# One first load in place of two, and the first casts dealt out anew, in a fused LoRA kernel

## The chip, the core and the metric

The kernel runs on one core of a Trainium2 chip. The metric is the device time of one execution in microseconds (us). Before the change it is 123.47 us, the median of 3 runs (123.42 to 123.6).

The engines are called as the profile calls them: PE (TensorE, matrix products), DVE (VectorE), ACT (ScalarE), POOL (GpSimd) and SP (SyncE, which here only issues DMAs and waits). PEld is the loading of weights on PE. Sixteen DMA engines move data between the chip's memory (HBM) and the core's on-chip memory.

## The reference

```python
def setup_inputs():
    batch, seq, d_model, r = 16, 512, 768, 16
    ...
def reference(x, A, B, scale):
    lora = np.matmul(np.matmul(x, A), B)
    return (x + scale * lora).astype(np.float32)
```

x is 8192 rows of 768 float32 numbers (25.2 MB), A is 768 x 16, B is 16 x 768, scale is 0.5. The result has the shape of x. So 25.2 MB come in and as many go out, and the arithmetic between is small: two products over a rank of 16, and one addition.

## The kernel before, in words

**Tiles.** The 8192 rows are 64 tiles of 128 rows. `PARTS = [9, 7, 16, 16, 16]` deals them into five parts; in a part of S tiles, each of the 128 partitions holds S rows that lie one behind the other in HBM, so a transfer of n tiles moves n x 3072 bytes in one piece per partition. `x_all` has room for the first 48 tiles in float32; the last part (16 tiles) takes the place of parts 0 and 1 when their results have been stored. The sum is made in place in `x_all`, and stored from there.

**Groups.** Compute goes in 8 groups of 8 tiles. In each group:

1. ACT and POOL cast ("narrow") four tiles each from float32 `x_all` to float16 `xn` (`narrowed`, line 194). ACT takes the first four tiles of a group, POOL the last four. In the first group this is dealt otherwise: POOL casts tiles 0 and 1, ACT tiles 2 and 3, then tiles 4 to 7.
2. DVE turns `xn` into `xt` (`turned`, line 250): a transpose of 32 x 32 blocks, so that the model dimension comes to lie across partitions. One instruction turns all eight tiles; in the first group there are two of four tiles each.
3. PE multiplies `xt` by A's weights `w_bd` into `ps_yt` (`projected`, line 281, 24 matmuls).
4. ACT scales that into `y_bd` (line 238, four instructions).
5. PE multiplies `y_bd` by B's weights `b_mm` into `lora_ps` (`raised`, line 302), for four pairs of tiles.
6. DVE adds each pair to `x_all` (`summed`, line 255, four instructions).

PE's program overlaps neighbouring groups, and semaphores tie the engines together. `s_first` and `s_narrow` count casts, `s_turned` turns, `s_y` and `s_spread` the steps 3 and 4, `s_lora` finished pairs. ACT casts its tiles of the next group (line 234) before it does step 4 of the present one, and the casts wait until PE has begun to read the turned tiles of the group before (`s_taken`).

**Weights.** A comes by three small DMAs into 12 rows of `a_rows`, DVE turns them (`a_t`, line 243), POOL casts them into `w_one` (line 214) and copies that four times into the block weights `w_bd` (line 220). B comes by one DMA into every fourth row of `b_rows`. POOL casts it to `b_half` (line 212). PE spreads it with the matrix `pick` (line 315, two matmuls, before anything else on PE), and ACT casts the result to `b_mm` (line 231). DVE's wait ahead of line 243 is on `s_a`, which counts A's three loads and POOL's cast of tiles 0 and 1. PE's first projection waits for `w_bd` (`s_w`, line 320) and then for the turned group (`s_turned`, line 321).

**Transfers.** All DMAs are issued by SP, in the order of its program, on one queue. `LOADS` lists the loads of x as (part, first tile, tiles). SP issues loads 0 and 1, waits until POOL has cleared `a_rows` (line 153), issues A's three, waits until POOL has cleared `b_rows`, issues B's, and then loads 2 to 5 without a wait. Each load has a semaphore of its own, and a cast waits for the load that its tiles come by. The first store (9 tiles, line 170) waits for ten finished pairs of tiles (line 169), though its sums are done earlier; the second (7 tiles) goes with it. The two loads of part 4 wait until these stores have landed (lines 172 to 175). The store of part 2 waits for the sixth group's step 5 to begin (`s_raise`, line 181); the last two stores wait for their sums.

Of the kernel before, what the change touches and what calls it, by code (L numbers as in the profile page):

```python
# [18 lines left out]
SUB = 4  # L19
# [5 lines left out]
SETS, SET = 3, 4  # L25
# [3 lines left out]
def kernel(  # L29
# [25 lines left out]
    def sb(name, shape, dtype):  # L55
        return nc.alloc_sbuf_tensor(name, shape, dtype).ap()
# [13 lines left out]
    b_rows = sb("b_rows", [P, D], fp32)  # L70
    b_half = sb("b_half", [P, D], MM_DT)
# [11 lines left out]
    def sem(name):  # L83
        sems.append(nc.alloc_semaphore(name))
        return sems[-1]
# [10 lines left out]
    def memory(t2, i, s, n):  # L96
        S = PARTS[i]
        return t2[ds(parts[i], S * P), :].rearrange("(p s) d -> p s d", s=S)[:, ds(s, n), :]

    def held(i, s, n):  # L100
        return tiles(where.index((i, s)), n)

    def tiles(t, n):
        return x_all[:, ds(t % ROOM, n), :]

    LOADS = [
        (0, 0, 2), (0, 2, 7), (1, 0, 7), (2, 0, 8), (2, 8, 8), (3, 0, 16), (4, 0, 8), (4, 8, 8)
    ]
    s_load = [sem(f"s_load{k}") for k in range(len(LOADS))]

    def load_of(t):
        i, s = where[t]
        return next(k for k, ld in enumerate(LOADS) if ld[0] == i and ld[1] <= s < ld[1] + ld[2])

    assert SETS * SET == NC
    s_a, s_b = sem("s_a"), sem("s_b")
    s_ready, s_brows, s_pick = sem("s_ready"), sem("s_brows"), sem("s_pick")
    s_w, s_bh, s_bp, s_bm = sem("s_w"), sem("s_bh"), sem("s_bp"), sem("s_bm")
    s_first, s_narrow, s_turned, s_taken = sem("s_first"), sem("s_narrow"), sem("s_turned"), sem("s_taken")
# [16 lines left out]
    def on_sync(e):  # L136
        def load(k):
            ld = LOADS[k]
            e.dma_start(out=held(*ld), in_=memory(x2, *ld)).then_inc(s_load[k], 16)  # L139

        def summed(k):
            e.wait_ge(s_sum, sorted(set(STORED)).index(STORED[k]) + 1)
            if STORED[k] + 1 < NG:

                e.sem_inc(s_free[PAIRS - 1], 1)

        def store(k, done):
            st = STORES[k]
            e.dma_start(out=memory(out2, *st), in_=held(*st)).then_inc(done, 16)

        load(0)
        load(1)
        e.wait_ge(s_ready, 1)
        blocks = A.rearrange("(c e) r -> c (e r)", e=64)
        for c in range(SETS):
            e.dma_start(
                out=a_rows[c : SET * SET : SET, :], in_=blocks[ds(c * SET, SET), :]
            ).then_inc(s_a, 16)
        e.wait_ge(s_brows, 1)
        e.dma_start(out=b_rows[0 : R * APART : APART, :], in_=B).then_inc(s_b, 16)  # L160
        for k in range(2, len(LOADS) - 2):
            load(k)

        for p in range(2, PAIRS):
            e.sem_inc(s_free[p], 1)
        summed(0)


        e.wait_ge(s_lora, 2 * PAIRS + 2)
        store(0, s_out0)  # L170
        store(1, s_out1)
        e.wait_ge(s_out0, 16)
        load(len(LOADS) - 2)
        e.wait_ge(s_out1, 16)
        load(len(LOADS) - 1)
        for k in range(2, len(STORES)):
            summed(k)
            if k == 2:


                e.wait_ge(s_raise, 6)
            store(k, s_out)
# [3 lines left out]
    def narrowed(e, copy, g, first, n=SUB):  # L186
        t = g * GROUP + first
        for k in dict.fromkeys(load_of(t + k) for k in range(n)):
            if (e, k) not in here:
                here.add((e, k))  # L190
                e.wait_ge(s_load[k], 16)
        if g:
            e.wait_ge(s_taken, g)
        ins = copy(out=xn[:, ds(first, n), :], in_=tiles(t, n))  # L194

        ins.then_inc(s_narrow if g else s_first if first else s_a, 1)

    def on_gpsimd(e):
        e.memset(a_rows[0:Q], 0.0).then_inc(s_ready, 1)  # L199
        e.memset(b_rows, 0.0).then_inc(s_brows, 1)  # L200
        e.memset(pick, 0.0).then_inc(s_pick, 1)
        e.memset(w_bd.rearrange("p c k m -> p (c k m)").bitcast(fp32), 0.0)  # L202
        e.memset(y_bd.rearrange("p s m -> p (s m)").bitcast(fp32), 0.0).then_inc(s_ready, 1)  # L203
        e.wait_ge(s_pick, 1)
        e.affine_select(  # L205
            out=pick, in_=pick, compare_op=mybir.AluOpType.not_equal, fill=1.0, base=0,
            pattern=[[0, NQ], [-APART, Q]], channel_multiplier=1,
        ).then_inc(s_pick, 1)
        narrowed(e, e.tensor_copy, 0, 0, SUB // 2)
        e.wait_ge(s_pick, 2)  # L210
        e.wait_ge(s_b, 16)
        e.tensor_copy(out=b_half, in_=b_rows).then_inc(s_bh, 1)  # L212
        e.wait_ge(s_ready, 3)
        e.tensor_copy(  # L214
            out=w_one.rearrange("i (c e) k r -> i c e (k r)", c=SETS),
            in_=a_t[0:Q].rearrange("i k r (e c) -> i c e (k r)", c=SET)[:, 0:SETS, 0:SET, :],
        ).then_inc(s_w, 1)
        e.wait_ge(s_w, 1)
        for b in range(NQ):
            e.tensor_copy(  # L220
                out=w_bd[ds(b * Q, Q), :, :, ds(b * Q, R)], in_=w_one
            ).then_inc(s_w, 1)
            e.wait_ge(s_w, b + 2)
        for g in range(1, NG):
            narrowed(e, e.tensor_copy, g, SUB)

    def on_scalar(e):
        narrowed(e, e.copy, 0, SUB // 2, SUB // 2)
        narrowed(e, e.copy, 0, SUB)
        e.wait_ge(s_bp, 1)  # L230
        e.copy(out=b_mm, in_=lora[0][:, 0, :]).then_inc(s_bm, 1)  # L231
        for g in range(NG):
            if g + 1 < NG:
                narrowed(e, e.copy, g + 1, 0)
            e.wait_ge(s_y, g + 1)
            for b in range(NQ):
                q = ds(b * Q, Q)
                last = e.mul(out=y_bd[q, :, q], in_=y_ps[q, :, :], mul=sc)  # L238
            last.then_inc(s_spread, 1)

    def on_vector(e):
        e.wait_ge(s_a, SETS * 16 + 1)
        e.transpose(  # L243
            out=a_t[0:Q].rearrange("i k r c -> i (k r) c"),
            in_=a_rows[0:Q].rearrange("c (i k r) -> c (k r) i", k=2, r=R),
        ).then_inc(s_ready, 1)

        def turned(first, n):
            ts = [v[:, ds(first, n), :].bitcast(fp32) for v in (xt, xn)]
            return e.transpose(out=ts[0], in_=ts[1])  # L250

        def summed(g, p):
            xs = tiles(g * GROUP + 2 * p, 2)
            e.wait_ge(s_lora, g * PAIRS + p + 1)
            ins = e.tensor_tensor(out=xs, in0=xs, in1=lora[p % 2], op=mybir.AluOpType.add)  # L255
            if p + 1 == PAIRS and g in STORED:
                ins.then_inc(s_sum, 1)
            elif g + 1 < NG or p + 2 < PAIRS:
                ins.then_inc(s_free[p], 1)

        for h in range(2):
            e.wait_ge(s_first, h + 1)
            ins = turned(h * SUB, SUB)
        ins.then_inc(s_turned, 1)
        for g in range(NG):
            if g + 1 < NG:
                e.wait_ge(s_y, g + 1)
                e.wait_ge(s_narrow, 2 * (g + 1))  # L268
                turned(0, GROUP).then_inc(s_turned, 1)
            for p in range(PAIRS):  # L270
                summed(g, p)

    def on_tensor(e):
# [58 lines left out]
        for p in range(PAIRS):  # L332
            raised(p)

    on_sync(nc.sync)
    on_gpsimd(nc.gpsimd)
    on_scalar(nc.scalar)
    on_vector(nc.vector)
    on_tensor(nc.tensor)

# [43 lines left out]
```

## Time and profile before

| what | value |
|---|---|
| time, median of 3 runs | 123.47 us (123.42 to 123.6) |
| time of the profiled execution | 123.43 us |
| its span, first to last instruction | 121.6 us |
| mean granted PE clock | 0.91 |
| busy: PE, PEld | 49.8 us (41%), 29.2 us (24%) |
| busy: DVE, ACT, POOL | 81.7 us (67%), 37.4 us (31%), 28.4 us (23%) |
| HBM read, HBM written | 25.26 MB, 25.17 MB |
| DVE sums (line 255) | 32 of 1735 ns, 53.7 us |
| DVE turns of x (line 250) | 9, 27.1 us |
| ACT casts of x (line 194) | 9, 23.4 us |
| POOL casts of x (line 194) | 8, 20.7 us |

The profile is one execution. The span runs from the first to the last recorded instruction; the time of the execution is some 1.8 us longer. An engine's busy time is that of its instructions, without waits. The profile has a list of the costliest groups of instructions (line, engine, operation, what is written from what, how many), a chain of waits that is followed back from the last instruction, a list of the instructions in order of time, and tables that give busy time, DMA share and GB/s for any stretch of the span. In rows of the list in order of time, the first number is the start in us from the span's beginning, the second the length in us, and what stands in square brackets is how long the engine had been idle and what ended that.

### The profile page before, as it was taken

Reading aid. Unit: us, or ns where it says so; the run is one execution under the profiler, and the core shown is the slowest. Engines: PE = TensorE matmul, PEld = TensorE weight load, DVE = VectorE, ACT = ScalarE, POOL = GpSimd, SP = SyncE. Lnnn points to the kernel's source line nnn. Section 1 sums busy time; section 2 is a strip of 40 time slices with the busy share of each in tenths; the row PEclk is TensorE's granted clock in tenths of the full one; section 3 lists DMA queues with packets and bytes.
Section 4 is the critical chain, followed back from the end, with each engine's and each line's share of the span. In section 5 each row is a group of like instructions: output and inputs, shape, how many; then the busy total and the mean of one; then the engine's idle time right before and its main releaser. Section 6 shows DMA issues by size and latency. Waiting matters only on the chain.

```text
span 121.6 us, 884 instructions
## 1 busy us (share of the span) xinstructions
PE 49.8 (41%) x322; PEld 29.2 (24%) x322; DVE 81.7 (67%) x42; ACT 37.4 (31%) x43; POOL 28.4 (23%) x24
## 2 busy tenths in 40 slices
PE   0000209487457547746745734774674320000000
PEld 0000006253223424424423322442442110000000
DVE  0000970599999999999999989999995990000000
ACT  4000967626408312735340093643004000000000
POOL 7730567126009002605300080620000000000000
PEclk9999999999999999999999999999999995555555
DMA  3999999999999897999999999998999899899890
GB/s 63 437 431 457 446 398 469 404 420 469 437 517 420 356 517 336 427 421 410 446 416 436 428 428 485 420 517 372 404 517 404 372 517 404 372 517 404 372 517 0
DMA packets 1928, 50.43 MB, mean 415 GB/s; under 512 B 236, under 2 KB 236, under 8 KB 392
## 3 DMA queue, kind: packets, MB, share of 16 engines
q1 hardware_dynamic: 1928, 50.43, 97.0%
HBM read 25.26 MB, written 25.17 MB: 415 GB/s over the span
## 4 chain that ended last, share of the span: by engine, by line
DVE 33%; DMA 29%; PE 9%; ACT 6%; POOL 2%; issue 2%; SPq 0%; DVEq 0%
DVE x_sb L255 21%; DMA x_sb<-in_x_dram 20%; DVE xt L250 12%; DMA out_dram<-x_sb 9%; PE ps_yt L281 6%; ACT xn L194 3%; PE lora_ps L302 3%; ACT y_bd L238 2%; POOL xn L194 2%; SPq L139 0%; SPq L379 0%; DVEq L268 0%; SPq L134 0%
## 5 line engine op out<-in xcount | busy, mean ns | idle before, releaser
L255 DVE TENSOR_TENSOR x_sb<-x_sb,lora_ps 128x1536 f32<-128x1536 f32 x32 | 53.7, 1735 | 1.4 <-PE lora_ps L302 1.4
L194 ACT CAST xn<-x_sb 128x3072 f16<-128x3072 f32 (+1 forms) x9 | 23.4, 2609 | 35.9 <-DMA x_sb<-in_x_dram 24.8
L302 PE MATMUL lora_ps<-b_mm,y_bd 128*128 128x512 f16 (+1 forms) x128 | 25.0, 328 | 22.6 <-ACT y_bd L238 14.3
L194 POOL CAST xn<-x_sb 128x3072 f16<-128x3072 f32 (+1 forms) x8 | 20.7, 2586 | 43.9 <-DMA x_sb<-in_x_dram 24.6
L250 DVE STREAM_TRANSPOSE xt<-xn 128x3072 f32<-128x3072 f32 (+1 forms) x9 | 27.1, 3006 | 5.3 <-PE ps_yt L281 4.4
L281 PE MATMUL ps_yt<-xt,w_bd 128*128 128x256 f16 x192 | 25.2, 282 | 12.2 <-DVE xt L250 12.2
L281 PEld LDWEIGHTS ps_yt<-xt,w_bd 128*128 128x128 f16 x192 | 18.5, 99 | 19.7 <-issue 15.4
L302 PEld LDWEIGHTS lora_ps<-b_mm,y_bd 128*128 128x128 f16 x128 | 10.6, 97 | 35.5 <-ACT y_bd L238 16.6
L238 ACT ACTIVATE y_bd<-ps_yt 32x256 f16<-32x256 f32 x32 | 12.0, 374 | 18.7 <-PE ps_yt L281 18.4
L243 DVE STREAM_TRANSPOSE a_t<-a_rows 32x1024 f32<-32x1024 f32 x1 | 2.0, 1955 | 12.2 <-DMA a_rows<-in_A_dram 12.2
L315 PE MATMUL lora_ps<-b_half,pick 128*128 128x512 f16 (+1 forms) x2 | 0.8, 500 | 13.5 <-POOL b_half L212 13.5
L315 PEld LDWEIGHTS lora_ps<-b_half,pick 128*128 128x128 f16 x2 | 0.1, 105 | 13.5 <-issue 13.5
L212 POOL CAST b_half<-b_rows 128x768 f16<-128x768 f32 x1 | 0.8, 827 | 5.5 <-DMA b_rows<-in_B_dram 5.5
L220 POOL COPY w_bd<-w_one 32x384 f16<-32x384 f16 x4 | 2.0, 500 | 0.2
L194 ACT ACT_TABLE_LOAD x1 | 1.3, 1283 | 0.9 <-SPq L134 0.9
L202 POOL MEMSET w_bd<- 128x1536 f32 x1 | 1.4, 1372 | 0.0
L214 POOL CAST w_one<-a_t 32x384 f16<-32x384 f32 x1 | 0.9, 857 | 0.9 <-DVE a_t L243 0.9
L199 POOL MEMSET a_rows<- 32x1024 f32 x1 | 0.9, 941 | 0.5 <-SPq L134 0.5
L231 ACT CAST b_mm<-lora_ps 128x768 f16<-128x768 f32 x1 | 0.8, 798 | 0.0
L200 POOL MEMSET b_rows<- 128x768 f32 x1 | 0.7, 728 | 0.0
L203 POOL MEMSET y_bd<- 128x512 f32 x1 | 0.5, 514 | 0.0
L205 POOL TENSOR_SCALAR_AFFINE_SELECT pick<-pick 128x128 f16<-128x128 f16 x1 | 0.3, 298 | 0.0
(5 smaller groups left out, 0.6 us busy)
## 6 DMA issues: line engine op xcount, KB each, us to landing
out_dram<-x_sb SPq DMA_DIRECT2D x3, 6144.0 KB, 20.1
x_sb<-in_x_dram SPq DMA_DIRECT2D x4, 3072.0 KB, 17.6
x_sb<-in_x_dram SPq DMA_DIRECT2D x1, 6144.0 KB, 41.6
x_sb<-in_x_dram SPq DMA_DIRECT2D x2, 2688.0 KB, 12.4
out_dram<-x_sb SPq DMA_DIRECT2D x1, 3456.0 KB, 11.5
out_dram<-x_sb SPq DMA_DIRECT2D x1, 2688.0 KB, 17.7
x_sb<-in_x_dram SPq DMA_DIRECT2D x1, 768.0 KB, 4.5
a_rows<-in_A_dram SPq DMA_DIRECT2D x3, 16.0 KB
```

The costliest lines, as they stand in the source:

```text
L194: ins = copy(out=xn[:, ds(first, n), :], in_=tiles(t, n))
L199: e.memset(a_rows[0:Q], 0.0).then_inc(s_ready, 1)
L202: e.memset(w_bd.rearrange("p c k m -> p (c k m)").bitcast(fp32), 0.0)
L214: e.tensor_copy(out=w_one.rearrange("i (c e) k r -> i c e (k r)", c=SETS), in_=a_t[0:Q].rearrange("i k r (e c) -> i c e (k r)", c=SET)[:, ...
L220: e.tensor_copy(out=w_bd[ds(b * Q, Q), :, :, ds(b * Q, R)], in_=w_one).then_inc(s_w, 1)
L238: last = e.mul(out=y_bd[q, :, q], in_=y_ps[q, :, :], mul=sc)
L243: e.transpose(out=a_t[0:Q].rearrange("i k r c -> i (k r) c"), in_=a_rows[0:Q].rearrange("c (i k r) -> c (k r) i", k=2, r=R),).then_inc(s_r ...
L250: return e.transpose(out=ts[0], in_=ts[1])
L255: ins = e.tensor_tensor(out=xs, in0=xs, in1=lora[p % 2], op=mybir.AluOpType.add)
L281: mm = e.matmul(y_ps, w_bd[:, c, k, :], xv[:, :, c, :, k], start=(m == 0), stop=(m == MMS - 1),)
L302: mms.append(e.matmul(t[:, k, ds(n0, w)], y_bd[:, 2 * p + k, :], b_mm[:, ds(n0, w)], start=True, stop=True,))
L315: last = e.matmul(lora[0][:, 0, ds(n0, w)], pick.rearrange("p b r -> p (b r)"), b_half[:, ds(n0, w)], start=True, stop=True,)
```

## The change

Four things are edited.

- `LOADS` begins with one load of nine tiles, (0, 0, 9), in place of (0, 0, 2) and (0, 2, 7). SP issues it, then goes on as before.
- The first group is cast like the others: ACT tiles 0 to 3, POOL tiles 4 to 7, one instruction each. The first of DVE's two turns waits for ACT's cast (`s_first`), the second for POOL's, which now counts on `s_narrow`; so the later waits on `s_narrow` are one higher.
- The cast of `b_rows` to `b_half` moves from POOL to ACT, behind ACT's cast of tiles 0 to 3.
- DVE's wait ahead of the turn of A counts A's three loads alone.

```diff
     LOADS = [
-        (0, 0, 2), (0, 2, 7), (1, 0, 7), (2, 0, 8), (2, 8, 8), (3, 0, 16), (4, 0, 8), (4, 8, 8)
+        (0, 0, 9), (1, 0, 7), (2, 0, 8), (2, 8, 8), (3, 0, 16), (4, 0, 8), (4, 8, 8)
     ]
...
         load(0)
-        load(1)
         e.wait_ge(s_ready, 1)
...
-        for k in range(2, len(LOADS) - 2):
+        for k in range(1, len(LOADS) - 2):
             load(k)
...
-        ins.then_inc(s_narrow if g else s_first if first else s_a, 1)
+        ins.then_inc(s_narrow if g or first else s_first, 1)
...
     def on_gpsimd(e):
...
-        narrowed(e, e.tensor_copy, 0, 0, SUB // 2)
-        e.wait_ge(s_pick, 2)
-        e.wait_ge(s_b, 16)
-        e.tensor_copy(out=b_half, in_=b_rows).then_inc(s_bh, 1)
+        narrowed(e, e.tensor_copy, 0, SUB)
         e.wait_ge(s_ready, 3)
...
     def on_scalar(e):
-        narrowed(e, e.copy, 0, SUB // 2, SUB // 2)
-        narrowed(e, e.copy, 0, SUB)
+        narrowed(e, e.copy, 0, 0)
+        e.wait_ge(s_b, 16)
+        e.copy(out=b_half, in_=b_rows).then_inc(s_bh, 1)
         e.wait_ge(s_bp, 1)
...
     def on_vector(e):
-        e.wait_ge(s_a, SETS * 16 + 1)
+        e.wait_ge(s_a, SETS * 16)
...
         for h in range(2):
-            e.wait_ge(s_first, h + 1)
+            e.wait_ge(s_narrow if h else s_first, 1)
             ins = turned(h * SUB, SUB)
...
                 e.wait_ge(s_y, g + 1)
-                e.wait_ge(s_narrow, 2 * (g + 1))
+                e.wait_ge(s_narrow, 2 * (g + 1) + 1)
                 turned(0, GROUP).then_inc(s_turned, 1)
```

## The prediction

> **What bounds the kernel now.** I read the page's DMA lines first, then the chain of waits, then the opening in order of time. The page, and below it the table of stretches (length, busy time of PE, PEld, DVE, ACT, POOL, then PE clock, DMA share, GB/s):
>
> ```profile
> span 121.6 us, 884 instructions
> ...
> DMA packets 1928, 50.43 MB, mean 415 GB/s; under 512 B 236, under 2 KB 236, under 8 KB 392
> ...
> q1 hardware_dynamic: 1928, 50.43, 97.0%
> ```
> ```profile
> 2.20:119.20 117.00, 49.83 (x322) 29.19 (x322) 81.74 (x42) 36.16 (x42) 26.97 (x19) 0.92 1.00 430
> 119.20:121.60 2.40, 0.00 (x0) 0.00 (x0) 0.00 (x0) 0.00 (x0) 0.00 (x0) 0.50 0.00 0
> ```
>
> The reader is to see one number: from 2.2 to 119.2 us the share of the 16 DMA engines is 1.00, while no compute engine is busy for more than 81.74 of these 117 us. The packet records of the trace (start, duration, size) say the same: at every point sampled from 3 to 119 us, 16 packets are in flight. So the profiled time is a sum: 1.98 us until the first packet, 118.25 us until the end of the last one (120.22), 1.39 us to the span's end (121.61), and 1.82 us outside the span, together 123.43. The median shown is 123.47, 0.04 above.
>
> The chain of waits tells another story (DVE 33%, DMA 29%), and must be read with care:
>
> ```profile
> 44.45 11.48 DMA out_dram<-x_sb
> 55.93 0.02 issue
> 55.95 13.71 DMA x_sb<-in_x_dram
> 69.66 0.05 issue
> 69.71 2.76 POOL xn L194
> ```
>
> It names work that released other work, not work that the full DMA engines waited for. The question for every edit is therefore twofold: does it change what the DMA engines must do, and does it delay the issue of a transfer until an engine runs dry?
>
> **The change on the DMA engines.** Loads (0,0,2) and (0,2,7) become one load (0,0,9). In the packet records each load is 128 packets, one a partition, eight to an engine. The small load's are 6144 B at 234 ns (median), the next one's 21504 B at 799 ns. The new ones are 27648 B; the store of the same tiles has packets of that size at 1025 ns, and 21504 B in 799 ns is the same rate. An engine thus does 8 x 1.025 = 8.20 us instead of 8 x (0.234 + 0.799) = 8.26, and one 9 ns semaphore write less: **-0.07 us**, with nothing to hide it, since the engines are the bound.
>
> Then the start. The 6144 B packets averaged 318 ns, not 234: 8 x 0.084 = 0.67 us per engine lost as the transfers begin. By the order of starts and ends, about 0.50 of it lies in each engine's first packet and 0.17 in the next ones. A first 27648 B packet may pay all of it again (0), or cover all of it (-0.67); a longer first load could also start worse, which I bound by one more such first packet (+0.50), though no row points there. I expect the first packet's loss to stay and half of the rest to go: **-0.08**. Sum on the DMA engines: -0.15.
>
> SP issues one DMA less: its two took 0.85 us from 0.97, and then it waits for GpSimd's clearing of a_rows, done at 1.89. With one it waits from 1.4, so A's loads go out at 1.92 as before, and all behind them too. The long first load keeps the engines busy until about 10.8; every later load is in the queue by 6.65.
>
> **The change on the compute engines.** The opening of before:
>
> ```profile
> 5.57 1.46 POOL L194 CAST xn<-x_sb 128x1536 f16<-128x1536 f32 x1 [0.73 <-DMA x_sb<-in_x_dram]
> 12.12 4.13 ACT L194 CAST xn<-x_sb 128x1536 f16<-128x1536 f32 x2 [9.93 <-DMA x_sb<-in_x_dram]
> 12.23 1.96 DVE L243 STREAM_TRANSPOSE a_t<-a_rows 32x1024 f32<-32x1024 f32 x1 [12.23 <-DMA a_rows<-in_A_dram]
> 12.52 0.83 POOL L212 CAST b_half<-b_rows 128x768 f16<-128x768 f32 x1 [5.49 <-DMA b_rows<-in_B_dram]
> ...
> 14.12 1.72 DVE L250 STREAM_TRANSPOSE xt<-xn 128x1536 f32<-128x1536 f32 x1
> 14.25 0.86 POOL L214 CAST w_one<-a_t 32x384 f16<-32x384 f32 x1 [0.90 <-DVE a_t L243]
> 15.17 2.18 POOL L220 COPY w_bd<-w_one 32x384 f16<-32x384 f16 x4
> ...
> 16.28 1.78 DVE L250 STREAM_TRANSPOSE xt<-xn 128x1536 f32<-128x1536 f32 x1 [0.44 <-ACT xn L194]
> ```
>
> - ScalarE: a two-tile and a four-tile cast (4.13) become one of four tiles, 2.75 by the later rows: 12.12 to 14.87. Behind it now stands the wait for B (landed by 12.52) and the cast of b_half, 0.80 by ScalarE's cast of the same shape (L231): done 15.70. PE's two matmuls on it take 0.8 to 1.0, then b_mm 0.8: 17.5. The next ScalarE cast waits for PE's first projections, about 18.9, so 1.4 us are spare.
> - GpSimd: the two-tile cast at 5.57 and L212 go; a four-tile cast, 2.75 by the later rows, runs 12.15 to 14.90. Behind it stand w_one and w_bd, 3.10 from the one's start to the other's end: 18.0, against 17.35 before.
> - VectorE: A's turn as before, 12.23 to 14.19; dropping the wait for GpSimd's first cast (done at 7.03) gives nothing, for A itself lands last. The first turn now needs all four of ScalarE's tiles: 14.89 to 16.65, the second 16.65 to 18.42, against 18.07.
> - PE starts 0.14 behind the turn: 18.56 against 18.21. w_bd is 0.4 earlier and does not decide.
>
> So compute starts **0.35 us later**, and VectorE, busy nearly without a gap from 22.5 to 72.2, carries this on. What covers it:
> - The first store goes out at 44.80 instead of 44.45. In the packet records its packets begin at 46.47 on the first engine and 47.29 on the last, each within 3 ns of the end of that engine's previous load. At the start of the kernel 1.0 us passed from the issue at 0.97 to the first engine's packet and 1.7 to the last's; by that the store could have begun at 45.5 to 46.2. About **1.0 us is spare**, 0.35 is used.
> - The next loads wait for stores to land and are issued at 55.95 and 62.5, 6 us ahead of need.
> - At 69.68 both casts wait for a load, and VectorE then idles 0.38 us; there the delay ends. The store issued at 74.47 hangs on that load through ScalarE, not on VectorE.
>
> Cost: 0. Without the cover it would be 0.35. Total: 123.47 - 0.15 = **123.32**. Latest and earliest engine end 1.0 us apart, so +/-0.2 around this is chance.
>
> **The rivals.**
>
> *The start loses nothing any more* (chance 0.18). If the long first packets cover the whole 0.67 us, 123.47 - 0.07 - 0.67 = 122.73. For it: the loss is seen only where packets are short and first. Against: 0.50 of it looks like a wait before any byte moves.
>
> *The loss stays whole* (0.07): -0.07 or nothing, 123.4 to 123.47.
>
> *Each load costs a fixed gap* (0.02). The 768 KB load needed 4.5 us to landing, of which 1.8 are bytes at 430 GB/s; if 2.7 us passed for each transfer in turn, dropping one would give 120.8. Against: the next load's packets begin about 6 ns behind the semaphore write on the same engine, and the DMA share is 1.00. The Trainium skill (DMA: Bandwidth & Descriptors, Anatomy of one DMA) gives a fixed cost of about 2.0 us to each DMA from GpSimd's queue, chiefly the wait for the write's receipt; taken in series that would be 121.5, and the trace shows it overlapped.
>
> *GpSimd's longer cast holds up the turn of A* (0.13, slower). L243 took 1.96 us for 1024 elements a partition, 1.9 ns each, where L250 took 1.72 for 1536, 1.1 each: some 0.8 us too much, about the 0.83 that GpSimd cast beside it. If VectorE stood still meanwhile, it would now stand until 14.90; the turn of A would end at 16.1 to 16.9, the second x turn at 19.6 to 20.4, 1.5 to 2.3 late. It decides from the 1.0 us that the first store has spare. At 2.3 the store's packets could begin at 47.8 to 48.5: the four engines that are latest throughout (they start it at 47.2 to 47.3) lose 0.5, early ones 1.2 to 2.0 of which they have 0.8 in hand. So +0.5 to +1.1 for the whole, less 0.15: about 124.1. Against: L250 ran at 1.72 with GpSimd's L214 and L220 beside it, 1.78 with part of L220, and GpSimd's 0.83 for L212 is on the line through its 1.46 (1536 elements) and 2.75 (3072). A's turn reads every 32nd element, L250 its elements in a row, which may explain the 1.9 ns as well. The Trainium skill (SBUF — State Buffer, Who interferes with whom) says that VectorE and GpSimd exclude each other for whole instructions when VectorE works in a two-port mode or with two SBUF inputs, else not; a turn has one input, and the L250 rows agree with "not".
>
> **How the numbers follow.** Forecast 0.60 at 123.32, with 0.10 of it falling under 123.22 by chance, 0.02 over 123.72 and 0.48 between. 0.2%, 0.25 us, is about what a measurement of this kernel can tell from no change. Faster: 0.10 + 0.18 + 0.02 = 0.30. Same: 0.48 + 0.07 = 0.55. Slower: 0.02 + 0.13 = 0.15. The range goes from the rival start (122.73) to the forecast's upper side and a partial loss of the store's cover, 123.9; the two far cases, 0.15, lie outside.
>
> **What would show it.** DMA share 1.00 from 2.2 to 119; 128 packets under 8 KB fewer (264); ScalarE and GpSimd each with one cast of 2.75 from 12.1; L243 near 1.96; PE's first L281 at about 18.55; the first store at about 44.8. L243 over 2.5, or a DMA share under 1 around 46 to 48 us, would prove the slower rival. The first store later than 45.5, or packets of the first load much off 1.03 us, would make the prediction wrong.

## The result, and the profile after

The changed kernel takes **124.07 us** (median of 15 executions, 123.59 to 124.77), the kernel before in the same rounds 123.55 us (15 executions, 123.42 to 124.01). The ratio is 1.0042, 95% interval 1.0024 to 1.0061: slower, where 123.32 us and no measurable change were forecast. Not only the middle moved: 14 of the 15 executions of before lie within 0.26 us, those of the changed kernel are spread over 1.2 us. The profiled execution took 123.84 us.

The page of the changed kernel, the same lines as shown of before:

```profile
span 122.0 us, 881 instructions
...
DMA packets 1784, 50.43 MB, mean 413 GB/s; under 512 B 220, under 2 KB 220, under 8 KB 248
...
q1 hardware_dynamic: 1784, 50.43, 96.8%
```

And its table of stretches, from 2.2 to 119.2 us (columns as before; the last two are DMA share and GB/s):

```profile
2.20:119.20 117.00, 50.88 (x322) 29.59 (x322) 81.65 (x42) 35.59 (x42) 27.39 (x18) 0.91 1.00 429
```

The reader is to see how little the view that carried the prediction shows: 144 packets fewer (128 of the small load, 16 semaphore writes), a DMA share of 1.00 as before, and 429 GB/s in place of 430. A share of 1.00 says that a packet is in flight on every engine, not that it moves at its usual pace.

The opening, in order of time:

```profile
12.09 1.95 DVE L240 STREAM_TRANSPOSE a_t<-a_rows 32x1024 f32<-32x1024 f32 x1 [12.09 <-DMA a_rows<-in_A_dram]
12.52 2.75 ACT L193 CAST xn<-x_sb 128x3072 f16<-128x3072 f32 x1 [10.32 <-DMA x_sb<-in_x_dram]
12.55 2.74 POOL L193 CAST xn<-x_sb 128x3072 f16<-128x3072 f32 x1 [7.70 <-DMA x_sb<-in_x_dram]
15.18 0.83 ACT L226 CAST b_half<-b_rows 128x768 f16<-128x768 f32 x1
...
15.30 3.44 DVE L247 STREAM_TRANSPOSE xt<-xn 128x1536 f32<-128x1536 f32 x2 [1.26 <-ACT xn L193]
```

The turn of A took 1.95 us although GpSimd cast beside it for longer, so the rival that it would be held up is refuted. But the casts begin at 12.52, not 12.12: the single load landed 0.4 us later than the two did in before's profile. PE's first projection and the first store follow (changed kernel, list in order of time):

```profile
18.89 4.65 PE L278 MATMUL ps_yt<-xt,w_bd 128*128 128x256 f16 x24 [1.94 <-DVE xt L247]
...
45.52 0.82 SPq L149 DMA_DIRECT2D out_dram<-x_sb  x2
```

The same rows of before:

```profile
18.21 4.26 PE L281 MATMUL ps_yt<-xt,w_bd 128*128 128x256 f16 x24 [3.92 <-DVE xt L250]
...
44.45 0.82 SPq L149 DMA_DIRECT2D out_dram<-x_sb  x2
```

So the store is 1.07 us late, where 0.35 had been expected: 0.68 at PE's start and 0.39 in the projection itself.

### The profile page after: what moved, and what is told of

The parts are those of the page before. It is cut to its first block, busy times and chain, and to the rows that moved or that the text cites. A ratio compares the mean times of both kernels' runs of the same rounds, so it can differ in the third digit from the quotient of the medians.

```text
span 122.0 us, 881 instructions
## 1 busy us (share of the span) xinstructions
PE 50.9 (42%) x322; PEld 29.6 (24%) x322; DVE 81.6 (67%) x42; ACT 36.9 (30%) x43; POOL 28.8 (24%) x23
## 4 chain that ended last, share of the span: by engine, by line
DVE 60%; DMA 9%; PE 6%; ACT 4%; issue 3%; SPq 0%
DVE x_sb L252 38%; DVE xt L247 22%; DMA x_sb<-in_x_dram 9%; PE ps_yt L278 5%; ACT xn L193 2%; PE lora_ps L299 1%; ACT y_bd L235 1%; SPq L376 0%; SPq L134 0%
## 5 line engine op out<-in xcount | busy, mean ns | idle before, releaser
L299 PE MATMUL lora_ps<-b_mm,y_bd 128*128 128x512 f16 (+1 forms) x128 | 25.6, 334 | 22.1 <-ACT y_bd L235 13.8
L193 POOL CAST xn<-x_sb 128x3072 f16<-128x3072 f32 x8 | 22.0, 2748 | 50.3 <-DMA x_sb<-in_x_dram 30.3
L193 ACT CAST xn<-x_sb 128x3072 f16<-128x3072 f32 x8 | 22.0, 2754 | 35.0 <-DMA x_sb<-in_x_dram 23.9
L226 ACT CAST b_half<-b_rows 128x768 f16<-128x768 f32 x1 | 0.8, 827 | 0.0
```

The lines of the kernel that those rows point to most:

```text
L299: mms.append(e.matmul(t[:, k, ds(n0, w)], y_bd[:, 2 * p + k, :], b_mm[:, ds(n0, w)], start=True, stop=True,))
```

## The experiments

Sixteen kernels ran, each with a profile and up to 12 times, beside executions of the kernel before on the same chip (medians 123.45 to 123.56 us). "Stretch" below is worked out from the packet records: the time that the packets of one transfer took over the median of their size, summed and divided by 16 engines.

Three theories: START (long first packets make single engines late, and the lateness stays), COVER (the late first store lets engines run dry), and from the run f0 on WINDOW (the first store has a best time of issue, and costs on both sides of it). The second store is issued right behind the first, both within 0.82 us, so every edit of the first store's wait moves the two together.

**e0_after: the changed kernel once more.** No edit.

> The changed kernel once more, for a second profile. Two theories. START: with 27648-byte packets the first ones take up to 1.2 us more than their steady 1.025 us (in the first profile up to 2.21 us), the engine that is hit worst is late by that much, and since all 16 engines do the same work without a pause, its lateness is still there at the end. COVER: the first store is issued late (45.5 us in the first profile, 1.1 us later than before), in the slower executions later than the spare 1 us allows, and engines run dry between 46 and 49 us. Both: median near 124.07 us, single times from 123.6 to 124.8. START: DMA share 1.00 from 46 to 49 us whatever the time, and the last packet of the first load ends at 12.0 us or later. COVER: if the profiled time is over 124.0, the store goes out at 46 us or later and the share from 46 to 49 us is under 0.97.

Measured: 123.97 us (123.43 to 125.26), ratio 1.0034 (1.0007 to 1.0062). The profiled execution was a short one, 123.51 us: casts from 11.89, the store at 45.02, the first load's last packet at 11.43 us. START's sign (that packet at 12.0 us or later) isn't there, but neither is a long execution to explain, and COVER had named a sign for long ones alone. It decides nothing.

**e1_split: the first load split again.** Changed kernel with

```diff
-        (0, 0, 9), (1, 0, 7), ...
+        (0, 0, 2), (0, 2, 7), (1, 0, 7), ...
...
         load(0)
+        load(1)
```

> The changed kernel with the first load split again into two tiles and seven; casts, waits and the cast of b_half stay as changed. START: back to 123.55 us, single times within 0.3 us of each other. COVER: the casts still wait for both loads, so compute is still some 0.4 to 0.8 us later than before; the time stays slower by 0.2 to 0.5 us and spread over 0.5 us or more.

Measured: 124.78 us (124.16 to 125.08), ratio 1.0088 (1.0063 to 1.0112), slower than either theory had it. ScalarE's first cast now waits for two loads. One of the waits, that for the seven tiles, is an instruction of its own, and ScalarE's table load stands behind it:

```profile
11.76 2.74 POOL L194 CAST xn<-x_sb 128x3072 f16<-128x3072 f32 x1 [6.92 <-DMA x_sb<-in_x_dram]
11.78 1.28 ACT L194 ACT_TABLE_LOAD   x1 [11.78 <-DMA x_sb<-in_x_dram]
...
13.07 2.75 ACT L194 CAST xn<-x_sb 128x3072 f16<-128x3072 f32 x1
```

As a test of the load this failed. But the store went out at 46.70 us, and the engines did run dry, for 0.8 us each on average; hardly a packet begins from 46.5 to 47.5 us (the last two numbers are DMA share and GB/s):

```profile
46.50:47.50 1.00, 0.17 (x1) 0.00 (x0) 1.00 (x1) 0.00 (x0) 0.00 (x0) 1.00 0.01 0
```

**e2_oneload: the single load alone.** Kernel before with the single load, the turn of A freed from the cast, and GpSimd's first cast counted on `s_narrow`:

```diff
-        (0, 0, 2), (0, 2, 7), (1, 0, 7), ...
+        (0, 0, 9), (1, 0, 7), ...
...
-        ins.then_inc(s_narrow if g else s_first if first else s_a, 1)
+        ins.then_inc(s_first if not g and first else s_narrow, 1)
...
-        e.wait_ge(s_a, SETS * 16 + 1)
+        e.wait_ge(s_a, SETS * 16)
...
+        e.wait_ge(s_narrow, 1)
         for h in range(2):
             e.wait_ge(s_first, h + 1)
...
-                e.wait_ge(s_narrow, 2 * (g + 1))
+                e.wait_ge(s_narrow, 2 * (g + 1) + 1)
```

> The kernel before with the single load of nine tiles; casts as before (GpSimd tiles 0 and 1 and b_half, ScalarE tiles 2 and 3, then 4 to 7), and the turn of A no longer behind GpSimd's cast. START: as slow as the changed kernel, 123.9 to 124.2 us, spread by 0.5 us or more. COVER: first projection at about 18.6 to 18.9 us, store at 44.9 to 45.3; mostly inside the spare, so 123.5 to 123.75 us.

Measured: 124.15 us (123.76 to 124.9), ratio 1.0052 (1.0033 to 1.0072). Inconclusive: this kernel's executions spend 2.3 us (median) outside the span, all others 1.8, for a reason that no run shows. By the spans it is 121.95 against 121.7, 0.25 us slower. Casts from 12.09, store at 45.44.

**e3_early_store: the changed kernel, first store behind eight pairs.**

```diff
-        e.wait_ge(s_lora, 2 * PAIRS + 2)
+        e.wait_ge(s_lora, 2 * PAIRS)
```

> The changed kernel with the first store's wait lowered from ten finished pairs to eight, so that it goes out as soon as its sums are done, near 43.5 us, some 2 us earlier. START: no gain, 124.07 us and the same spread. COVER: the slow executions go; 123.5 to 123.85 us, spread under 0.3 us.

Measured: 123.93 us (123.41 to 124.42), ratio 1.0032 (1.0016 to 1.0048). As START had it; but the records show something new. The store went out at 43.22, and the last load's packets, at other times 1.82 us, took up to 2.90: a stretch of 0.59 us per engine, where the profiles with the store at 44.4 us or later have none. What was won on one side may have been lost on the other.

**e4_long_first: seven tiles first, then two.** Kernel before with

```diff
-        (0, 0, 2), (0, 2, 7), (1, 0, 7), ...
+        (0, 0, 7), (0, 7, 2), (1, 0, 7), ...
```

> The kernel before with the sizes of its first two loads exchanged, seven tiles and then two: as many packets, the same casts, and no cast can start later than before. START (long packets at the beginning cost lateness on single engines, which stays to the end): 123.8 to 124.1 us, spread over 0.5 us, first packets of 21504 bytes up to 1 us longer than 0.80. COVER (the first store is late and engines run dry between 46 and 49 us): 123.55 us and as narrow as before, the store at 44.5 us or earlier.

Measured: 123.49 us (123.36 to 123.69), ratio 0.9997 (0.9984 to 1.001). The first packets of 21504 bytes took up to 2.12 us, as START wanted, and the time didn't move: START fell here. The store went out at 44.27.

**e5_split_swap: the change without its single load.** As e1_split, with the first group's halves exchanged:

```diff
     def on_gpsimd(e):
-        narrowed(e, e.tensor_copy, 0, SUB)
+        narrowed(e, e.tensor_copy, 0, 0)
...
     def on_scalar(e):
-        narrowed(e, e.copy, 0, 0)
+        narrowed(e, e.copy, 0, SUB)
```

> The changed kernel with the first load split into two tiles and seven, as in e1_split, and with the first group's halves exchanged (GpSimd tiles 0 to 3, ScalarE 4 to 7), so that ScalarE waits for one load alone and the profile of e1_split's 1.28 us table load behind its wait cannot return. START: 123.5 to 123.6 us, narrow. COVER: compute still starts some 0.3 us later than before; the store at 44.8 to 45.6 us, depending on PE's clock in its first projection; mostly covered, a few executions over 124.0, median 123.55 to 123.8.

Measured: 123.62 us (123.36 to 123.81), ratio 1.0008 (0.9996 to 1.002). Casts from 11.73, projection at 18.20, store at 45.33. That lies in COVER's range and only 0.02 us above START's, so it separates neither.

**e6_both: e5_split_swap with the store behind eight pairs** (the edit of e3_early_store).

> e5_split_swap with the first store's wait lowered to eight pairs as in e3_early_store. Both theories together leave nothing late: 123.45 to 123.55 us, no execution over 123.9. If the time stays over 123.8, neither theory holds the cause.

Measured: 123.99 us (123.69 to 124.17), ratio 1.0036 (1.0023 to 1.005): a miss, and the most useful one. With nothing late the time went up. Store at 42.91; the last load's stretch is 0.85 us per engine. COVER alone doesn't hold either.

**e7_one_eight: e6_both with loads of one and eight tiles.**

```diff
-        (0, 0, 2), (0, 2, 7), (1, 0, 7), ...
+        (0, 0, 1), (0, 1, 8), (1, 0, 7), ...
```

> e6_both with the first loads split into one tile and eight: first packets of 3072 bytes. START: the shorter the first packets, the less is lost: 123.4 to 123.55 us. COVER: no difference from e6_both.

Measured: 123.97 us (123.56 to 124.24), ratio 1.0041 (1.0026 to 1.0056). Store at 43.58, last load's stretch 0.57. START had 123.4 to 123.55 us: first packets of half the size gained nothing over e6.

**f0_before_early: only the store's time, earlier.** Kernel before with the edit of e3_early_store.

> The kernel before with one edit: the first store waits for eight pairs in place of ten, issued near 42.5 us. A third theory, WINDOW, has formed from e1, e3, e6 and e7: the time hangs on when the first store is issued against the end of the loads; queued too early it stretches the last load's packets (up to 2.9 us in place of 1.8, 0.55 to 0.85 us per engine), too late the engines run dry. WINDOW: 123.9 to 124.1 us. START (only the first load's packets matter): 123.5 us.

Measured: 124.06 us (123.93 to 124.53), ratio 1.0046 (1.0031 to 1.0061). One wait, in a kernel that is otherwise before's, costs as much as the whole change. The intervals 44 to 50, 46.5 to 47.5 and 54 to 63 us, first of before, then of f0_before_early:

```profile
44.00:50.00 6.00, 3.66 (x26) 2.05 (x25) 6.00 (x4) 2.22 (x1) 2.19 (x1) 1.00 0.94 403
46.50:47.50 1.00, 0.95 (x9) 0.58 (x8) 1.00 (x2) 0.00 (x0) 0.00 (x0) 1.00 0.91 387
54.00:63.00 9.00, 5.03 (x36) 2.96 (x34) 9.00 (x6) 4.25 (x5) 2.75 (x1) 1.00 0.98 414
```
```profile
44.00:50.00 6.00, 3.66 (x26) 2.24 (x26) 6.00 (x4) 1.07 (x1) 1.04 (x1) 1.00 0.91 329
46.50:47.50 1.00, 0.95 (x8) 0.50 (x6) 1.00 (x2) 0.00 (x0) 0.00 (x0) 1.00 0.19 83
54.00:63.00 9.00, 5.72 (x41) 3.41 (x39) 9.00 (x6) 4.25 (x5) 2.75 (x1) 1.00 0.98 423
```

A packet counts in the interval in which it begins. From 44 to 50 us the share hardly differs (0.94 and 0.91), the rate does (403 and 329 GB/s): the engines are busy with packets that take longer. Few begin from 46.5 to 47.5 because those before them last up to 2.96 us; the stretch of the last load is 1.10 us per engine.

**f1_before_late1: only the store's time, later.** Kernel before with

```diff
+    s_pad = sem("s_pad")
...
         e.wait_ge(s_lora, 2 * PAIRS + 2)
+        for _ in range(16):
+            e.sem_inc(s_pad, 1)
```

> The kernel before with 16 empty semaphore increments ahead of the first store on SyncE, so that it goes out some 0.6 to 1.2 us later, as in the changed kernel; nothing else is touched. WINDOW: between 123.6 and 124.2 us and spread like the changed kernel's, the later the more. START: 123.5 us, narrow.

Measured: 123.99 us (123.59 to 124.51), ratio 1.0034 (1.0019 to 1.0049): size and spread of the change, from one delay. In before's profile the store went out 21.98 us after the first projection's end; by that distance the increments delay it by 0.95 us here (projection's end 22.02, store at 44.95).

```profile
44.00:50.00 6.00, 3.69 (x27) 2.40 (x28) 6.00 (x4) 2.29 (x1) 2.26 (x1) 1.00 0.94 403
46.50:47.50 1.00, 0.95 (x8) 0.42 (x6) 1.00 (x2) 0.00 (x0) 0.00 (x0) 1.00 1.04 442
54.00:63.00 9.00, 5.14 (x36) 3.16 (x36) 9.00 (x6) 4.25 (x5) 2.75 (x1) 1.00 0.97 401
```

No engine runs dry at 46.5. In this profile a loss shows where the second store gives way to the next load: 401 GB/s against 414 from 54 to 63 us. That store's packets are stretched by 0.32 us per engine (before: 0.16), and one engine lost so much there that it started the next store at 77.55 us, 1.25 after the middle one, and was last to the end. But the next store, too, was issued later, at 75.39 us in place of 74.47, and ahead of it up to eight engines were without a packet between 75.9 and 76.3 us (0.11 us per engine on average; before: none). So this profile isn't free of dry engines; the one that ended last wasn't among them.

**f2_before_late2: the store held until PE begins the next projection.** Kernel before with

```diff
         e.wait_ge(s_lora, 2 * PAIRS + 2)
+        e.wait_ge(s_taken, 4)
```

> The kernel before, the first store held until PE has begun the fourth group's projection, near 46.2 us, 1.7 us later. WINDOW: near e1_split, 124.4 to 124.9 us, DMA share under 0.9 from 44 to 50 us. START: 123.5 us.

Measured: 124.73 us (124.54 to 125.28), ratio 1.0098 (1.0079 to 1.0117). Store at 46.95:

```profile
44.00:50.00 6.00, 3.66 (x25) 1.97 (x23) 6.00 (x4) 2.19 (x1) 2.16 (x1) 1.00 0.79 338
46.50:47.50 1.00, 1.00 (x10) 0.86 (x11) 1.00 (x1) 0.00 (x0) 0.00 (x0) 1.00 0.01 0
```

Here the engines are dry, and share and rate fall together. When the store comes they all start within 0.15 us of each other (47.80 to 47.94), and the second store's stretch is 0.67 us per engine.

**f3_after_nine: the changed kernel, first store behind nine pairs.**

```diff
-        e.wait_ge(s_lora, 2 * PAIRS + 2)
+        e.wait_ge(s_lora, 2 * PAIRS + 1)
```

> The changed kernel with the first store's wait lowered from ten pairs to nine, some 0.7 us earlier, 44.3 to 45.2 us, where the kernel before has it. Single load, casts and all else as changed. WINDOW: the loss goes, 123.5 to 123.65 us and narrow. START: 123.9 to 124.1 us, spread as in the changed kernel.

Measured: 123.54 us (123.44 to 124.19), ratio 1.0008 (0.9996 to 1.002). Single load, casts and all other waits as changed, only the store back at 44.26: the loss is gone from the median, though two of the eleven executions took 123.98 and 124.19.

**g1, g2: 8 and 32 increments in place of f1's 16.**

> f1_before_late1 with 8 increments in place of 16: the first store some 0.25 us later than before. If lateness costs in proportion, between before and f1: 123.6 to 123.8 us. If there is a threshold (engines dry), 123.5 us. If the increments themselves cost, and not the lateness, also near f1, 123.9 us.

> f1_before_late1 with 32 increments: some 1.0 us later than before, near 45.5 us, where the changed kernel's first profile has it. In proportion: 124.2 to 124.5 us. With a threshold at about 45.6 us: as f1, 124.0 us, with a few executions over 124.5.

Measured: g1 123.72 us (123.37 to 124.6), ratio 1.0023 (1.0005 to 1.0042); g2 124.85 us (124.45 to 125.43), ratio 1.0108 (1.0085 to 1.0131). By the distance from the projection's end the delays are 0.48 and 1.89 us, not 0.25 and 1.0: an increment takes some 59 ns, which I had put at half. g2 thus repeats f2 (1.88 us late) with another way of waiting, and the two agree. The cost doesn't wait until engines run dry at the first store: it is there at 0.48 us. Between 0.48 and 0.95 us the intervals overlap; at 1.89 it is clearly larger.

**g3_split_swap_nine: e5_split_swap with the store behind nine pairs** (the edit of f3_after_nine).

> e5_split_swap with the first store behind nine pairs, 44.0 to 44.8 us: the casts of the change without its single load, and the store where the kernel before has it. WINDOW: 123.45 to 123.55 us. If the casts cost by themselves, it stays at 123.62 or above.

Measured: 123.53 us (123.37 to 123.67), ratio 0.9997 (0.9984 to 1.001). Store at 44.22. No cost of the new casts alone is seen.

**g4_before_nine: kernel before, store behind nine pairs.**

> The kernel before with the first store behind nine pairs, near 43.7 us: between f0_before_early (42.3 us, 124.06) and before. WINDOW: 123.6 to 123.9 us, the last load's packets stretched by 0.2 to 0.6 us per engine.

Measured: 123.45 us (123.37 to 124.1), ratio 1.0003 (0.9991 to 1.0014). Store at 43.90, last load's stretch 0.12. A miss: 123.6 to 123.9 us and a stretch of 0.2 to 0.6 had been expected, and 0.6 us earlier costs nothing that can be measured. No version beat the kernel before.

## Why the prediction was wrong

The kernels that differ from before in the store's time alone, in the order of that time (delay as worked out under f1, from the projection's end):

| kernel | store against before | store issued, us | ratio (95% interval) | last load's stretch, us | second store's stretch, us |
|---|---|---|---|---|---|
| f0 | 1.9 us earlier | 42.28 | 1.0046 (1.0031 to 1.0061) | 1.10 | 0.01 |
| g4 | 0.6 earlier | 43.90 | 1.0003 (0.9991 to 1.0014) | 0.12 | 0.19 |
| before | 0 | 44.45 | 1 | 0.00 | 0.16 |
| g1 | 0.5 later | 44.74 | 1.0023 (1.0005 to 1.0042) | 0.00 | 0.27 |
| f1 | 0.95 later | 44.95 | 1.0034 (1.0019 to 1.0049) | 0.00 | 0.32 |
| f2 | 1.9 later | 46.95 | 1.0098 (1.0079 to 1.0117) | 0.00, then dry | 0.67 |
| g2 | 1.9 later | 46.87 | 1.0108 (1.0085 to 1.0131) | 0.00, then dry | 0.66 |

Issue times and stretches are those of one profiled execution, the ratios those of many.

- **The step that failed: "Cost: 0."** A gain of 0.15 us was forecast, a loss of 0.52 measured. The step priced the delay by asking only whether engines run dry at the first store, and took the 1.0 us until then as free. f1 and g1 show that it isn't: delays of 0.95 and 0.48 us, with no engine dry at that store in either profile, cost 0.34% and 0.23%. In f1 some engines were dry 30 us later, at the next store, which the prediction hadn't counted either; in the changed kernel's profile and in g1's none were.
- **The delay itself was too small: 0.35 us.** For the casts it was near: with the loads split, the first projection begins at 18.09 to 18.23 in four profiles of the new casts (e5, e6, e7, g3; mean 18.18) and at 17.64 to 18.21 in seven of before's (mean 17.86), 0.32 later. The single load came on top: in five profiles with it ScalarE's first cast begins at 12.19 on average (11.89 to 12.52), in twelve with two loads at 11.75 (11.56 to 12.12; e4 left out, and for e1, with its table load in the way, GpSimd's cast taken). In four profiles of the changed kernel's opening (first profile, e0, e3, f3) the projection begins at 18.58 on average, 0.72 after before's. The profile of before that I worked from was itself a late one, 18.21. The prediction had named a first store later than 45.5 us as a sign that it was wrong; in the first profile it went out at 45.52.
- **What moves the store from one execution to the next** is PE's first projection as well: 4.15 to 5.28 us for the same 24 matmuls. In the trace's records of single matmuls these start 213 ns apart up to a certain moment (the first interval is shorter), and some 110 ns apart after it. In before's profile that moment is 21.2 us, behind 13 intervals of 213 ns; in the changed kernel's first profile it is 22.7, behind 17; in f1 20.7, behind 12; in e1, e2, e5, e7 and g2 all 24 keep the slow pace. The Trainium skill (TensorE: Matmul & The Clock Gate, Part 1) says that PE runs at half clock until a window of about 3.4 us of activity has passed, and that the windows run on regardless of the kernel's start; by that rule the first projection's length changes from run to run. The trace agrees: the pace about doubles, and after different times. The profile's row of the clock shows full speed from the start, but its records of the clock begin only at that moment (21.24 us in before, 22.72 in the changed kernel).
- **"-0.07"** nearly stands by the records (the new load's packets took 1.027 to 1.032 us at the median, not 1.025, which makes it -0.06 to -0.02), but is too small to be told apart: f3, which has the single load, agrees with before within its interval.
- **"-0.08" at the start didn't come.** The first load's packets lost 0.60 us per engine in the first profile of the changed kernel, 0.65, 0.71 and 0.70 in e0, e3 and f3, against 0.67 in the profile that I worked from and 0.51 to 0.68 (mean 0.59) in seven with before's loads. The first packets took up to 2.21 us in the first profile and 2.56 in e3, in place of 1.03, and the load's last packet ended at 12.03 in the first profile, against 11.54 in before's. That this costs more than the late landing isn't seen: e4's first packets took up to 2.12 us and its time didn't move.
- **The rival that ended slower** had the place right, the first store, and the wrong cause, the turn of A, which stayed at 1.95 us. Its price began at 1.0 us of delay, too far out.

Shown, for the median of many executions: the time at which the two stores are issued makes a loss and a spread of the change's kind (f0, f1, f2, g1, g2), and setting it back undoes the loss in the changed kernel (f3). Its size fits: PE started 0.72 us late on average, between g1's delay and f1's, and the change's 0.42% (0.24 to 0.61) overlaps with the costs of both. A single execution isn't settled by the issue time: e0's profile has the store at 45.02 us and took 123.51, f1's has it at 44.95 and took 124.12. Only seen beside it, not separated: that on the late side the loss lies in the second store's packets. Against it stands e5, whose second store was stretched by 0.38 us per engine in an execution of 123.69. In f2 and g2, where all engines had started together, these packets are stretched most; why being in step should cost is open, as is why a store that is queued early slows the last load's packets. A way to stagger the engines with the issue time held fixed wasn't tried.

## What to carry to other kernels

A full DMA share is no proof that a delay is free: look at the rate and at single packets where loads give way to stores, and back. When a transfer's issue hangs on a compute chain, its time may have a best value, as here; before pricing any edit ahead of it, measure that curve by shifting this issue alone. And read more than one profile of the kernel before: here its opening varied by as much as the whole expected effect.

## What the runs showed of the hardware that was not expected

- A store queued 1.9 us earlier behind the same load stretched that load's last packets from 1.82 to as much as 2.96 us (f0). Packets of the second store, 0.80 us each, took up to 1.60, just double, among its last ones, where the next load followed (before and the runs that delay the store).
- Idle engines began the store 0.85 to 0.99 us after its issue (e1, f2: issued at 46.70 and 46.95, first packets at 47.55 to 47.69 and 47.80 to 47.94).
- An empty semaphore increment on SyncE takes about 59 ns, an estimate from the delays (16 of them 0.95 us, 32 of them 1.89).
- With two waits ahead of ScalarE's first cast, its table load of 1.28 us ran behind the first of them, at 11.78 us, in place of at 0.91 (e1).
